# Average pooling of 2x2x2: contiguous loads of 3 MB with unequal read and write pieces in place of channel rows of 32 KB

## The chip, the cores and the metric

The kernel runs on one core of a Trainium2 chip. The metric is device microseconds (us) of one execution, median of several. A comparison of two kernels is a ratio: the mean time of one kernel's fast runs over that of the other's in the same rounds, with a 95% interval; it is therefore not quite the ratio of the medians.

## The reference

`x` is 8 x 32 x 32 x 32 x 32 float32 (33.55 MB), the output 8 x 32 x 16 x 16 x 16 (4.19 MB):

```python
window = x[:, :, d_s:d_s + 2, h_s:h_s + 2, w_s:w_s + 2]
result[:, :, i, j, k] = np.mean(window, axis=(-3, -2, -1))
```

Two neighbouring planes of 4 KB (32 x 32 floats) give one output plane of 1 KB. Any even number of planes can be pooled by itself, so a partition may hold any such piece of any channel.

## The kernel before

There are 256 channels, two sets `t` of 128, one channel per partition. A unit `k` is 1 KB of a channel (KF = 256 floats); a channel has 128 of them. A load takes 32 KB of each of 128 channels (the channels lie 128 KB apart in HBM), or twice 16 KB at the end. VectorE adds pairs along d, w and h, and the result waits in `obuf` for four stores.

```python
KF = 256
xv = x.rearrange("b c d h w -> (b c) (d h w)")
pool_in = ctx.enter_context(tc.tile_pool(name="pin", bufs=5))
obuf = [pool_out.tile([P, 16 * KF], F32, name=f"obuf{t}") for t in range(2)]
plan = [
    (0, 0, (32,)), (0, 32, (32,)), (0, 64, (32,)), (0, 96, (32,)),
    (1, 0, (32,)), (1, 32, (32,)), (1, 64, (16, 16)), (1, 96, (16, 16)),
]
def pool_unit(buf, t, k0, kb):
    # ... (cut: views)
    nc.vector.tensor_add(out=..., in0=a[:, :, 0], in1=a[:, :, 1])      # d
    nc.vector.tensor_add(out=c, in0=bv[:, :, 0], in1=bv[:, :, 1])      # w
    nc.vector.tensor_tensor_reduce(out=obuf[t][...], ...)              # h, and 1/8
for t, k0, parts in plan:
    tin = pool_in.tile([P, 32 * KF], F32, tag="tin", name="tin")
    # ... (cut: one dma_start per part, then pool_unit per part)
    nc.sync.dma_start(
        out=v, in_=xv[t * P:(t + 1) * P, (k0 + o) * KF:(k0 + o + kb) * KF])
for queue, t, k0, kb in [
    (nc.scalar, 1, 0, 2), (nc.sync, 0, 0, 16),
    (nc.sync, 1, 2, 12), (nc.sync, 1, 14, 2),
]:
    queue.dma_start(
        out=ov[t * P:(t + 1) * P, k0 * KF:(k0 + kb) * KF],
        in_=obuf[t][:, k0 * KF:(k0 + kb) * KF])
# ... (cut: the first load is moved ahead of the opening barrier, the closing
# waits for the stores are rebuilt; the change leaves both as they are)
```

## Time and profile before

| | before |
|---|---|
| median | 91.75 us (3 runs); 91.81 us in 6 runs beside the changed kernel |
| first data packet starts | 1.01 us |
| last data packet ends | 90.03 us |
| bytes moved | 33.55 MB in, 4.19 MB out |
| VectorE busy | 64.1 us of 86.6 |

The view to begin with is the DMA row of the page: it is full from the start to the end (a DMA share of 0.99 to 1.01 from 12.1 to 85.2 us), so any gain must come from making the 16 DMA engines' work smaller or their holes fewer. The profile's lines are in the prediction. Beyond the page, I use the **packet records** of the trace (start, duration, size of every packet on the 16 engines); durations of single packets and the moments of each engine's semaphore write are from there. (The semaphore writes are records of 4 bytes and 9 ns. Before there are 14 x 16 of them, so 16 for each load and store; I count one per engine, and take a transfer as landed with the last of its 16: before, that of the first load starts at 11.74, and VectorE starts on the load at 12.12. The records don't number the engines.)

### The profile page before, as it was taken

The numbers are of one execution on the slowest core, as the hardware profiler recorded it, in microseconds if no ns is written. First come the engines' busy times: TensorE is split into PE (matmuls) and PEld (weight loads), VectorE is DVE, ScalarE is ACT, GpSimd is POOL, SyncE is SP. The second block draws the span as 40 slices with busy tenths as digits, with TensorE's granted clock in tenths as the row PEclk, the third lists the DMA queues.
The fourth block names the chain that finished last, engine by engine and source line by source line (L and its number), as shares of the span: only waits on it lengthen the run. The fifth ranks groups of instructions, "written<-read, shape, count | busy, mean of one in ns | idle before, by whom it ended". The sixth has DMA issues, their size and how long they took to land.

```text
span 86.6 us, 91 instructions
## 1 busy us (share of the span) xinstructions
DVE 64.1 (74%) x40; POOL 0.2 (0%) x4
## 2 busy tenths in 40 slices
DVE  0000049993999749992999749992999999999994
POOL 0000000000000000000000000000000000000000
DMA  8889998899979999799988999699999999999999
GB/s 242 379 363 469 485 485 348 379 485 485 469 333 409 485 485 424 318 469 485 485 348 379 485 485 469 288 454 416 405 407 424 407 462 394 462 394 454 394 454 398
DMA packets 1774, 36.48 MB, mean 421 GB/s; under 512 B 192, under 2 KB 192, under 8 KB 320
## 3 DMA queue, kind: packets, MB, share of 16 engines
q1 hardware_dynamic: 1630, 36.22, 98.4%
q10 hardware_dynamic: 144, 0.26, 0.8%
HBM read 33.55 MB, written 4.19 MB: 436 GB/s over the span
## 4 chain that ended last, share of the span: by engine, by line
DMA 83%; DVE 14%; SPq 1%; issue 0%; DVEq 0%
DMA tin<-in_x_dram 83%; DVE tin L58 8%; DVE tin L62 4%; DVE obuf L65 2%; SPq L77 1%; DVE dummy L65 0%; DVEq L102 0%
## 5 line engine op out<-in xcount | busy, mean ns | idle before, releaser
L58 DVE TENSOR_TENSOR tin<-tin 128x4096 f32<-128x4096 f32 (+1 forms) x10 | 35.7, 3570 | 20.7 <-DMA tin<-in_x_dram 20.6
L62 DVE TENSOR_TENSOR tin<-tin 128x2048 f32<-128x2048 f32 (+1 forms) x10 | 18.6, 1865 | 0.3
L65 DVE CUSTOM_DVE_ANT_1 obuf<-tin 128x1024 f32<-128x1024 f32 (+1 forms) x10 | 10.1, 1011 | 0.3
L65 DVE DVE_READ_ACCUMULATOR2_ANT dummy<- 128x1 f32 x10 | 0.8, 82 | 0.0
L178 POOL MEMSET const-uint8-127<- 128x1 uint8 x1 | 0.1, 102 | 0.0
L178 POOL MEMSET const-bfloat16-1.0<- 128x1 bf16 x1 | 0.1, 101 | 0.0
L178 POOL MEMSET const-float32-0.0<- 128x1 f32 x1 | 0.1, 98 | 0.2 <-issue 0.2
L178 POOL MEMSET const-float32-1.0<- 128x1 f32 x1 | 0.1, 98 | 0.0
## 6 DMA issues: line engine op xcount, KB each, us to landing
tin<-in_x_dram SPq DMA_DIRECT2D x6, 4096.0 KB, 35.0
tin<-in_x_dram SPq DMA_DIRECT2D x4, 2048.0 KB, 38.9
out_dram<-obuf SPq DMA_DIRECT2D x1, 2048.0 KB, 36.8
out_dram<-obuf SPq DMA_DIRECT2D x1, 1536.0 KB, 8.8
out_dram<-obuf ACTq DMA_DIRECT2D x1, 256.0 KB, 9.9
out_dram<-obuf SPq DMA_DIRECT2D x1, 256.0 KB, 4.9
```

The costliest lines, as they stand in the source:

```text
L58: nc.vector.tensor_add(out=b.rearrange("p (o e) -> p o e", o=od), in0=a[:, :, 0], in1=a[:, :, 1])
L62: nc.vector.tensor_add(out=c, in0=bv[:, :, 0], in1=bv[:, :, 1])
L65: nc.vector.tensor_tensor_reduce(out=obuf[t][:, o0:o0 + od * 256].rearrange("p (j k) -> p j k", k=16), in0=cv[:, :, 0], in1=cv[:, :, 1], s ...
L77: nc.sync.dma_start(out=v, in_=xv[t * P:(t + 1) * P, (k0 + o) * KF:(k0 + o + kb) * KF])
L178: nc = _bacc.Bacc("TRN2", target_bir_lowering=False, num_devices=1)
```

## The change

The input is treated as one flat array. A load takes 3 MB in one piece, 24 KB per partition (six planes), the last 2 MB; eleven loads in place of ten, six buffers in place of five. Then, after scheduling, the access patterns of the sources are rewritten by hand: a load reads 64 rows of 48 KB, although it writes 128 rows of 24 KB; a store reads 15 or 12 KB of a partition at once, although it writes 5 or 4 pieces of 3 KB. The first load is left with 24 KB reads. The intent is fewer, larger reads per DMA engine, with the bytes unchanged.

```diff
-    pool_in = ctx.enter_context(tc.tile_pool(name="pin", bufs=5))
+    pool_in = ctx.enter_context(tc.tile_pool(name="pin", bufs=6))
     plan = [
-        (0, 0, (32,)), (0, 32, (32,)), ... (1, 96, (16, 16)),
+        (0, 24), (24, 24), (48, 24), (72, 24), (96, 24), (144, 24),
+        (120, 24), (168, 24), (192, 24), (216, 24), (240, 16),
     ]
-                out=v, in_=xv[t * P:(t + 1) * P, (k0 + o) * KF:(k0 + o + kb) * KF])
+            out=buf, in_=xf[P * k * KF:P * (k + kb) * KF].rearrange("(p e) -> p e", p=P))
-        (nc.scalar, 1, 0, 2), (nc.sync, 0, 0, 16), (nc.sync, 1, 2, 12), (nc.sync, 1, 14, 2),
+        (nc.scalar, 15, 1, 3), (nc.sync, 0, 5, 3), (nc.sync, 18, 4, 3), (nc.sync, 30, 1, 2),
     # ... (cut: destination of a store "(u p e) -> p u e", n pieces of kb units)
+    for n in copies[1:]:
+        # ... (cut)
+        if load:
+            ap = [[2 * row, 64], [1, 2 * row]]
+        else:
+            ap = [list(src.ap[0])] + [[1, 1]] * (len(src.ap) - 2) + [[1, size]]
+        if ap != [list(d) for d in src.ap]:
+            program[n] = copy.replace(i, ins=[copy.replace(src, ap=ap)], ant_dge_precooked=False)
```

More of the change, by code (lines that the diff above doesn't have):

```diff
@@ L1 @@
+import copy
 from contextlib import ExitStack
@@ L26, in pool_rows @@
     add = mybir.AluOpType.add
-    xv = x.rearrange("b c d h w -> (b c) (d h w)")
-    ov = out.rearrange("b c d h w -> (b c) (d h w)")
-    pool_in = ctx.enter_context(tc.tile_pool(name="pin", bufs=5))
+    xf = x.rearrange("b c d h w -> (b c d h w)")
+    of = out.rearrange("b c d h w -> (b c d h w)")
+    pool_in = ctx.enter_context(tc.tile_pool(name="pin", bufs=6))
     pool_out = ctx.enter_context(tc.tile_pool(name="pout", bufs=1))
-    obuf = [pool_out.tile([P, 16 * KF], F32, name=f"obuf{t}") for t in range(2)]
+    obuf = [pool_out.tile([P, kb * KF], F32, name=f"obuf{t}") for t, kb in enumerate((15, 17))]
     dummy = pool_out.tile([P, 1], F32, name="dummy")
     plan = [
-        (0, 0, (32,)),
-        (0, 32, (32,)),
-        (0, 64, (32,)),
-        (0, 96, (32,)),
-        (1, 0, (32,)),
-        (1, 32, (32,)),
-        (1, 64, (16, 16)),
-        (1, 96, (16, 16)),
+        (0, 24),
+        (24, 24),
+        (48, 24),
+        (72, 24),
+        (96, 24),
+        (144, 24),
+        (120, 24),
+        (168, 24),
+        (192, 24),
+        (216, 24),
+        (240, 16),
     ]
@@ L69, in pool_unit @@
         )
-    for t, k0, parts in plan:
-        tin = pool_in.tile([P, 32 * KF], F32, tag="tin", name="tin")
-        views = []
-        o = 0
-        for kb in parts:
-            v = tin[:, o * KF:(o + kb) * KF]
-            nc.sync.dma_start(
-                out=v, in_=xv[t * P:(t + 1) * P, (k0 + o) * KF:(k0 + o + kb) * KF])
-            views.append((v, k0 + o, kb))
-            o += kb
-        for v, k, kb in views:
-            pool_unit(v, t, k, kb)
-    for queue, t, k0, kb in [
-        (nc.scalar, 1, 0, 2),
-        (nc.sync, 0, 0, 16),
-        (nc.sync, 1, 2, 12),
-        (nc.sync, 1, 14, 2),
-    ]:
+    for k, kb in plan:
+        tin = pool_in.tile([P, 24 * KF], F32, tag="tin", name="tin")
+        buf = tin[:, :kb * KF]
+        nc.sync.dma_start(
+            out=buf, in_=xf[P * k * KF:P * (k + kb) * KF].rearrange("(p e) -> p e", p=P))
+        t = int(k >= 120)
+        pool_unit(buf, t, k - 120 * t, kb)
+    for queue, k, n, kb in [
+        (nc.scalar, 15, 1, 3),
+        (nc.sync, 0, 5, 3),
+        (nc.sync, 18, 4, 3),
+        (nc.sync, 30, 1, 2),
+    ]:
+        t = int(k >= 15)
+        o = k - 15 * t
         queue.dma_start(
-            out=ov[t * P:(t + 1) * P, k0 * KF:(k0 + kb) * KF],
-            in_=obuf[t][:, k0 * KF:(k0 + kb) * KF],
+            out=of[P * k * KF:P * (k + n * kb) * KF].rearrange("(u p e) -> p u e", u=n, p=P),
+            in_=obuf[t][:, o * KF:(o + n * kb) * KF].rearrange("p (u e) -> p u e", u=n),
         )
@@ L103 @@
     blocks = nc.main_func.blocks
-    opening, program = blocks[0].instructions, blocks[tc.starting_block_idx].instructions
+    program = blocks[tc.starting_block_idx].instructions
+    copies = [n for n, i in enumerate(program) if isinstance(i, mybir.InstDMACopy)]
+    for n in copies[1:]:
+        i = program[n]
+        src = i.ins[0]
+        load = "in_" in src.memref
+        if load:
+            row = src.ap[-1][1]
+            assert src.ap == ((row, 128), (1, row)) and row <= 24 * KF
+            ap = [[2 * row, 64], [1, 2 * row]]
+        else:
+            size = src.ap[-1][1] * (src.ap[1][1] if len(src.ap) == 3 else 1)
+            ap = [list(src.ap[0])] + [[1, 1]] * (len(src.ap) - 2) + [[1, size]]
+        if ap != [list(d) for d in src.ap]:
+            program[n] = copy.replace(i, ins=[copy.replace(src, ap=ap)], ant_dge_precooked=False)
+    opening = blocks[0].instructions
     load = next(i for i in program if isinstance(i, mybir.InstDMACopy))
```

## The prediction

> **What bounds the kernel now.** I read the page first: busy shares, the 40 slices, the byte totals and the chain of waits.
>
> ```profile
> span 86.6 us, 91 instructions
> ## 1 busy us (share of the span) xinstructions
> DVE 64.1 (74%) x40; POOL 0.2 (0%) x4
> ...
> DMA  8889998899979999799988999699999999999999
> ...
> HBM read 33.55 MB, written 4.19 MB: 436 GB/s over the span
> ## 4 chain that ended last, share of the span: by engine, by line
> DMA 83%; DVE 14%; SPq 1%; issue 0%; DVEq 0%
> ```
>
> VectorE (DVE) is idle for a quarter of the span; the DMA row is full from the first slices to the last; the chain is 83% load traffic. The 436 GB/s is slightly flattering: the span closes with the last VectorE instruction, while the last store is still moving. So I asked for stretches that run past the span (start:end, length, DVE busy, POOL busy, clock, DMA share, GB/s):
>
> ```profile
> 12.10:59.80 47.70, 39.75 (x20) 0.00 (x0) 1.00 0.99 429
> 59.80:70.50 10.70, 9.80 (x4) 0.00 (x0) 1.00 1.01 417
> 70.50:85.20 14.70, 14.32 (x16) 0.00 (x0) 1.00 1.00 428
> 85.20:90.10 4.90, 0.26 (x2) 0.00 (x0) 1.00 0.89 375
> ```
>
> The 16 DMA engines stay at a share of 0.99 to 1.01 until 85.2, and go on until the last packet record ends at 90.03. The run takes 91.75, so 1.7 us lie after the last data packet and belong to no work that this change touches. The kernel is bound by DMA engine time from 1.0 us (first packet) to 90.0 us.
>
> The packet records give that time a formula. A 32 KB packet takes 1213 ns, 16 KB 611, 12 KB 460, 2 KB 84 (medians). From the ends: (1213-84)/(32768-2048) = 0.03675 ns per byte, which leaves 8.7 ns per packet; it reproduces 611 and 460. One engine has 37.75 MB / 16 = 2.359 MB, so 86.7 us are bytes. It has 48 packets of 32 KB, 40 of 16 KB, 8 of 12 KB and 16 of 2 KB, 112 in all: 0.97 us. The 14 semaphore writes of 9 ns add 0.13. Sum 87.8 us of the 89.0 that pass from the first packet to the last. The other 1.2 are the start (the first load's data end at 11.75 instead of 1.01 + 9.70 = 10.71, 1.0 us) and uneven engines at the end.
>
> [...] 1/0.03675 = 27.2 GB/s per engine, times 16 is 435. [...] The trace has such a cost, 8.7 ns, but since every transfer before reads and writes equal pieces, it cannot tell whether reads or writes are counted. [...]
>
> **The change part by part.** Bytes don't change: 86.7 us of engine time before and after, in a queue already full. Nothing in the new layout can shorten this term while the rate is 27.2 GB/s per engine.
>
> *Pieces, per engine.* Reads: the first load keeps rows of 24 KB (8), nine loads of 3 MB have 4 reads of 48 KB each (36), the last of 2 MB has 4 of 32 KB; the four stores read 8 each (32). Sum 80. Writes: eleven loads x 8 = 88; stores 8 x (1+5+4+1) = 88. Sum 176. At 8.7 ns each:
> - if reads are counted, 80 against 112: -0.28 us;
> - if writes are counted, 176 against 112: +0.56 us.
>
> One more load adds one 9 ns semaphore write.
>
> *VectorE.* The rows by shape give the unit times:
>
> ```profile
> L58 DVE TENSOR_TENSOR tin<-tin 128x4096 f32<-128x4096 f32 x6 | 26.6, 4426 | 20.6 <-DMA tin<-in_x_dram 20.6
> L62 DVE TENSOR_TENSOR tin<-tin 128x2048 f32<-128x2048 f32 x6 | 13.8, 2292 | 0.2
> L58 DVE TENSOR_TENSOR tin<-tin 128x2048 f32<-128x2048 f32 x4 | 9.1, 2286 | 0.1
> L65 DVE CUSTOM_DVE_ANT_1 obuf<-tin 128x1024 f32<-128x1024 f32 x6 | 7.3, 1224 | 0.2
> L62 DVE TENSOR_TENSOR tin<-tin 128x1024 f32<-128x1024 f32 x4 | 4.9, 1224 | 0.1
> L65 DVE CUSTOM_DVE_ANT_1 obuf<-tin 128x512 f32<-128x512 f32 x4 | 2.8, 692 | 0.1
> ```
>
> A 24 KB row is half-way between these shapes: (4426+2286)/2 = 3356, (2292+1224)/2 = 1758, (1224+692)/2 = 958, plus 82 for the accumulator read: 6.15 us per load. A 3 MB load takes the engines 4 x (49152 x 0.03675 + 8.7) = 7.26 us, so VectorE keeps up and idles 1.1 us per load.
>
> *The end.* First load: 1.0 + 1.0 (start) + 8 x 0.912 = 9.3. The tenth: 9.3 + 9 x 7.27 + 0.97 for ScalarE's store in between = 75.7. VectorE starts 0.4 us after data (before: 11.75 and 12.12), works from 76.1 to 82.25, then on the last 2 MB unit (4.28 us) to about 86.6, against 85.46 now. The engines meanwhile finish the last load at 80.6, the 15 KB store at 85.2, the 12 KB store at 88.9. The last store is issued at 86.6 and needs about 1.0 us to its first packet (the first load's lag): 87.6, so 1.3 us of slack, where before it was 2.4 (86.5 against 88.9). VectorE's later end should be hidden.
>
> *Buffers and issues.* Six buffers of 3 MB let five loads (36 us of traffic) be queued ahead; before, four of 4 MB (39 us). Issues take 0.33 to 0.53 us now; even at twice that the second is out long before 8 us, when engines first need it.
>
> **The rivals.** (1) *Writes are counted, not reads.* For it: nothing excludes it. Against: the change forces larger reads by hand while it lets writes shrink, which its author would hardly keep if writes counted. 92.3 us. (2) *VectorE becomes the end.* For: its last instruction moves 1.1 us later. Against: 1.3 us of slack is left. If loads land a microsecond late, or the issue lag is longer than at the start, the last store starves and the time is about 92 to 92.5. (3) *Contiguous HBM reads raise the rate.* Against: packets of 32 KB all take 1211 to 1215 ns in whole loads[...]. Only the 1.0 us at the start could shrink; at best 91.0. (4) *Unequal sides make an engine stall at each piece, or HBM takes 3 KB writes badly.* Nothing in this trace speaks for it; 10% on the stores' 9.9 us would be +1.0.
>
> **Range and chances.** I take reads as counted: 91.75 - 0.28 + 0.01 = 91.5 us. Low 91.0: the read saving and half of the loss at the start. High 92.3: writes counted. Even with no packet cost and no loss at the start, 91.75 - 0.97 - 1.0 = 89.8 would barely pass the 2% line at 89.9, so faster by over 2% gets 0.02. Slower by over 2% (above 93.6) needs rival 2 and 4 together: 0.04. Within 2%: 0.94.
>
> **What the changed profile would show.** Right: a DMA share near 1.0 throughout; 3 MB loads landing 7.26 to 7.30 us apart; shapes of 3356, 1758 and 958 ns; last VectorE end near 86.6; stores as fast as before although they write 3 KB. Reads counted: 48 KB and 15 KB packet records of 1815 and 573 ns. Writes counted: 24 KB and 3 KB records (912 and 122 ns), and a load of 7.30 us. The prediction is wrong if the DMA row has holes (engines waiting for VectorE or an issue), if a load lands faster than 7.2 us after the last (above 435 GB/s), or if the first load loses much more or less than 1.0 us.

The forecast's sum came to 91.75 - 0.28 + 0.01 = 91.5 us, with the 8.7 ns per packet and the 27.2 GB/s per engine (435 for 16) worked out from the packet records of the kernel before ("such a cost" is these 8.7 ns).

## The result, and the profile after

The changed kernel takes **92.31 us** (92.10 to 92.72, 6 runs), the kernel before 91.81 (91.72 to 91.97, 6 runs): ratio 1.0058, interval 1.0035 to 1.0081. It is 0.5 us slower, not 0.25 faster.

From the changed kernel's page:

```profile
span 88.4 us, 98 instructions
## 1 busy us (share of the span) xinstructions
DVE 65.0 (73%) x44; POOL 0.2 (0%) x4
...
DMA  8899999889988999889998899989999988998999
...
HBM read 33.55 MB, written 4.19 MB: 427 GB/s over the span
## 4 chain that ended last, share of the span: by engine, by line
DMA 78%; DVE 19%; SPq 1%; issue 0%; DVEq 0%
```

The bound is the same: a full DMA row. VectorE's share of the chain rose from 14 to 19% because the page's chain is followed back from the last VectorE instruction, and before that one VectorE now works through the last two loads back to back (76.9 to 87.3, where before it was the last one alone, 81.2 to 85.5); after it the engines are still storing, so this is not the end of the program. What matters is where the engines' time went, and two stretches show it.

**The start.** The DMA row of the first 12 us, before (40 slices of 0.3 us; a packet stands in the slice in which it starts):

```profile
DMA  0009990009900990099009920992079207920592
```

and changed:

```profile
DMA  0009901099799999999999959939959993039993
```

Before, the 16 engines move in step: all start a packet in the same one or two slices, then none does. Changed, they are spread out. The packet records say how far. Before, the engines' first packets end between 2.82 and 3.27 us; changed, between 2.46 and 3.55. With the first packet at 1.01 and 8 packets each, an undelayed first load would end at 1.01 + 8 x 1.213 = 10.71 before and 1.01 + 8 x 0.912 = 8.31 changed. The slowest engine's semaphore write comes at 11.74 and 9.92: **1.03 us late before, 1.61 changed**. The spread stays: the 16 semaphore writes of a load are spread over 0.43 us in the first and the third load before, and over 1.08 to 1.09 in each of the first eight loads changed. At the end the engines finish within 0.48 us of one another before (89.54 to 90.02) and within 0.84 changed (89.80 to 90.64). The last data packet ends at 90.64 instead of 90.03, and the two profiled executions took 92.44 and 91.76.

**The loads.** VectorE waits for each load, so its first instruction per load marks the landings. Start, duration, and in brackets the idle time before it, changed kernel:

```profile
10.30 3.36 DVE L62 TENSOR_TENSOR tin<-tin 128x3072 f32<-128x3072 f32 x1 [10.30 <-DMA tin<-in_x_dram]
17.57 3.36 DVE L62 TENSOR_TENSOR tin<-tin 128x3072 f32<-128x3072 f32 x1 [1.12 <-DMA tin<-in_x_dram]
24.87 3.36 DVE L62 TENSOR_TENSOR tin<-tin 128x3072 f32<-128x3072 f32 x1 [1.15 <-DMA tin<-in_x_dram]
32.17 3.36 DVE L62 TENSOR_TENSOR tin<-tin 128x3072 f32<-128x3072 f32 x1 [1.15 <-DMA tin<-in_x_dram]
39.48 3.36 DVE L62 TENSOR_TENSOR tin<-tin 128x3072 f32<-128x3072 f32 x1 [1.15 <-DMA tin<-in_x_dram]
```

The distance is 7.27 at first, then 7.30. My two formulas gave 4 x 1815 = 7.26 with reads counted and 8 x 912 = 7.30 with writes counted, plus a semaphore write. The packet records show the same turn: records of 48 KB (they are the reads: 64 per load beside 128 rows of 24 KB written, with 16 semaphore writes per load, and the result was correct) take 1815 ns until about 25 us, then 1824 to 1829.

### The profile page after: what moved, and what is told of

It is laid out like the page before. It is cut to its first block, busy times and chain, and to the rows that moved or that the text cites. A ratio compares the mean times of both kernels' runs of the same rounds, so it can differ in the third digit from the quotient of the medians.

```text
span 88.4 us, 98 instructions
## 1 busy us (share of the span) xinstructions
DVE 65.0 (73%) x44; POOL 0.2 (0%) x4
## 4 chain that ended last, share of the span: by engine, by line
DMA 78%; DVE 19%; SPq 1%; issue 0%; DVEq 0%
DMA tin<-in_x_dram 78%; DVE tin L62 10%; DVE tin L66 5%; DVE obuf L69 3%; SPq L78 1%; DVE dummy L69 0%; DVEq L104 0%
## 5 line engine op out<-in xcount | busy, mean ns | idle before, releaser
L62 DVE TENSOR_TENSOR tin<-tin 128x3072 f32<-128x3072 f32 (+1 forms) x11 | 35.9, 3260 | 21.6 <-DMA tin<-in_x_dram 21.6
L66 DVE TENSOR_TENSOR tin<-tin 128x1536 f32<-128x1536 f32 (+1 forms) x11 | 18.8, 1710 | 0.4
L69 DVE CUSTOM_DVE_ANT_1 obuf<-tin 128x768 f32<-128x768 f32 (+1 forms) x11 | 10.3, 934 | 0.4
```

The lines of the kernel that those rows point to most:

```text
L62: nc.vector.tensor_add(out=b.rearrange("p (o e) -> p o e", o=od), in0=a[:, :, 0], in1=a[:, :, 1])
L69: nc.vector.tensor_tensor_reduce(out=obuf[t][:, o0:o0 + od * 256].rearrange("p (j k) -> p j k", k=16), in0=cv[:, :, 0], in1=cv[:, :, 1], s ...
```

## The experiments

The theory has two parts. (A) The start is wider because of **where the 16 engines begin to read**. The rows of the first load lie 128 KB apart before and 24 KB apart changed. (No run here shows which engine reads which rows, so the distance between the engines' first rows is not known; the runs with moved rows test the pitch alone.) (B) **The slower side of a transfer sets the pace**, and in the 3 MB loads that is the write side. Rivals: reads are counted after all, the start is chance, or the contiguous layout, the small stores or the widening by hand cost time in themselves.

### Undo the widening of the loads

```diff
-            ap = [[2 * row, 64], [1, 2 * row]]
+            ap = [list(d) for d in src.ap]
```

> The changed kernel, but loads 2 to 11 read rows of 24 KB (16 KB in the last) as they write them; stores as changed. 40 more reads per engine, as many writes as before. If reads are counted everywhere at 8.7 ns: +0.35 us against the changed kernel (92.3), so 92.65. If writes are counted everywhere: 92.3. My theory, that the slower side sets the pace and in the loads of 3 MB that is the write side (48 KB records of 1824 to 1829 ns against 1815): packets of 912 ns, 0.0 to 0.1 us more than changed, 92.3 to 92.4. If the slower issue of the widened second load causes the wide start: first load lands evenly, 91.9.

Measured: 92.27 us, ratio to before 1.0048 (1.0030 to 1.0066), the changed kernel 1.0058. Forty more reads per engine cost nothing that can be measured. In the trace, on the mean of the engines, loads 2 and 3 of the changed kernel took 7.25 us, load 4 7.28, and the next ones 7.30; with the widening undone loads 2 to 4 took 7.27, load 5 7.28, and the next ones 7.30. Loads 2 to 8 together took 51.00 us in both: 28 reads fewer per engine saved nothing, where 8.7 ns each would be 0.24. The slower issue is no cause of the start either: with it gone (the second load's issue takes 0.34 us, in the changed kernel 0.56), the slowest engine ended the first load at 9.91, in the changed kernel at 9.92.

### Undo the widening of the stores

```diff
-            ap = [list(src.ap[0])] + [[1, 1]] * (len(src.ap) - 2) + [[1, size]]
+            ap = [list(d) for d in src.ap]
```

> The changed kernel, but stores read pieces of 3 KB as they write them; loads as changed. 56 more reads per engine, as many writes. If the store is paced by its reads: 9 x 121.5 - 573 - 466 = 55 ns per partition, 8 partitions per engine, +0.44 us: 92.75, and packet records of 3 KB at about 121 ns. If writes pace it: 92.3, no change.

Measured: 92.34 us, ratio 1.0054 (1.0039 to 1.0068). The trace has the expected records of 121 ns, but neighbouring ones overlap (the 40 per engine of the first large store take 4.70 us, 117.6 ns each). From the last load to the last store the engines need 9.13 us on the mean, changed kernel 8.93: 0.20 more, not 0.44, for 56 reads more and the same writes. The changed kernel's own tail fits reads as well: bytes (29 KB x 8 partitions x 0.03675 = 8.73) and 24 reads at 8.7 ns make 8.94; its 80 writes at 8.7 ns would make 9.43. That reads pace the stores rests on these two traces; the times don't show it (1.0054 and 1.0058).

### Double the writes of the loads

Loads 2 to 11 write two pieces of 12 KB per partition, first with reads of 48 KB, then with reads of 12 KB:

```diff
+                i = copy.replace(i, outs=[copy.replace(dst, ap=[[step, 128], [row // 2, 2], [1, row // 2]])])
 # first:  source  [[2 * row, 64], [1, 1], [1, 2 * row]]
 # second: source  [[row, 128], [row // 2, 2], [1, row // 2]]
```

> The changed kernel, but loads 2 to 11 write two pieces of 12 KB (8 KB in the last) per partition; reads stay at 48 KB. Theory that the write side paces the loads: one piece costs 8 to 11 ns beyond its bytes, so a load of 3 MB takes 16 x (451.6 + 8 to 11) = 7.35 to 7.40 us instead of 7.30, time 92.8 to 93.3. If only reads are counted: 7.26 us each, 92.3.

> The changed kernel, but loads 2 to 11 read and write pieces of 12 KB (8 KB in the last). Theory that the slower side paces: as with 48 KB reads and 12 KB writes within 0.02 us per load, 7.37 us, time 92.8 to 93.3. If each side's pieces cost and add up: 7.37 plus 16 x 8.7 = 7.5 us, 94.5.

Measured: 92.73 us (ratio 1.0102) and 92.78 us (1.0106). VectorE's first instructions of the first of the two:

```profile
10.19 3.36 DVE L62 TENSOR_TENSOR tin<-tin 128x3072 f32<-128x3072 f32 x1 [10.19 <-DMA tin<-in_x_dram]
17.55 3.36 DVE L62 TENSOR_TENSOR tin<-tin 128x3072 f32<-128x3072 f32 x1 [1.21 <-DMA tin<-in_x_dram]
24.93 3.36 DVE L62 TENSOR_TENSOR tin<-tin 128x3072 f32<-128x3072 f32 x1 [1.23 <-DMA tin<-in_x_dram]
32.31 3.36 DVE L62 TENSOR_TENSOR tin<-tin 128x3072 f32<-128x3072 f32 x1 [1.23 <-DMA tin<-in_x_dram]
39.68 3.36 DVE L62 TENSOR_TENSOR tin<-tin 128x3072 f32<-128x3072 f32 x1 [1.22 <-DMA tin<-in_x_dram]
```

and of the second:

```profile
24.92 3.36 DVE L62 TENSOR_TENSOR tin<-tin 128x3072 f32<-128x3072 f32 x1 [1.23 <-DMA tin<-in_x_dram]
32.30 3.36 DVE L62 TENSOR_TENSOR tin<-tin 128x3072 f32<-128x3072 f32 x1 [1.23 <-DMA tin<-in_x_dram]
39.67 3.36 DVE L62 TENSOR_TENSOR tin<-tin 128x3072 f32<-128x3072 f32 x1 [1.22 <-DMA tin<-in_x_dram]
```

Both land 7.38 us apart although one makes four times the reads of the other. Only the writes are the same in both, and they are what differs from the changed kernel's 7.30. **So the writes into SBUF set the pace of these loads.** In the first run a 48 KB read, which takes 1815 ns at first, takes 1842 to 1848 in steady state.

The distances of the landings (means over the engines) also give prices; the records don't, since they overlap by some 4 ns. A load of 3 MB took 7.253 us with 4 reads per engine (changed kernel, loads 2 and 3), 7.272 with 8 (widening undone, loads 2 to 4) and 7.310 with 16 (second run here, loads 2 and 3): **4.75 ns for each further read**. Later on, where the reads no longer mattered, it took 7.304 with 8 writes and 7.379 with 16: **9.4 ns for each further write**. So with equal pieces on both sides the write side is the slower one here (9.4 against 4.75 ns).

The turn has a size, too. Adding up how much sooner than the steady distance the loads before it landed gives 0.13 us in the changed kernel, 0.12 with the widening undone, 0.13 and 0.14 in the two runs here, although the steady distance is reached with load 3 in one and with load 6 in another. It looks as if the reads can get some 0.13 us ahead of the writes and must then keep their pace; fewer reads would only use up this lead sooner. That is an interpretation; the agreement of the four numbers is what speaks for it.

### Move the first load's rows

All four give a wrong result: only the addresses that the first load reads differ. First the changed kernel with its rows 128 KB apart, then 32 KB apart:

```diff
+        if k == 0:
+            src = xf.rearrange("(c e) -> c e", e=128 * KF)[:P, :kb * KF]   # then: e=32 * KF
```

> The changed kernel, but the first load takes its 128 rows of 24 KB at a pitch of 128 KB (wrong result on purpose). Theory: the wide spread of the engines' first packets (1.45 to 2.35 us) comes from where the 16 engines start to read; then the first load's data end by 9.4 instead of 9.9 us, and the time falls by 0.4 to 0.5 us to 91.85. Rival, that the start is chance or comes from the row size or the second load's issue: 92.3 as changed.

> The changed kernel, but the first load takes its rows of 24 KB at a pitch of 32 KB instead of 24 (wrong result on purpose): nearly contiguous[...]. Theory: the wide start comes from where the 16 engines start[...]; then the slowest engine's first load ends by 9.5 (as with a pitch of 128 KB), time 92.0. Rival: contiguity as such is bad; then 9.8 or later and 92.3.

Then the kernel before with a contiguous first load (rows 32 KB apart), and with rows 24 KB apart (32 KB long, so they overlap in HBM):

```diff
+            if t == 0 and k0 == 0:
+                src = ...   # rows of kb * KF floats, one every 32 * KF; then: one every 24 * KF
```

> The kernel before, but its first load takes a contiguous range of 4 MB (wrong result on purpose). Theory of the start: first packets spread over 0.8 us or more, first load's data end 0.4 to 0.6 us later than 11.75, time 92.2 to 92.4. Rival: 91.8 as before.

> The kernel before, but the first load takes its rows of 32 KB at a pitch of 24 KB (rows overlap in HBM, wrong result on purpose)[...]. Theory: the slowest engine's first load ends 0.4 to 0.6 us later than 11.75, time 92.2. Rival, that the row size or another part of the changed program makes the wide start: 91.8 as before.

| kernel | first load's pitch | slowest engine late by | ratio to before (interval) |
|---|---|---|---|
| before | 128 KB | 1.03 us | 1 |
| before, contiguous | 32 KB | 1.23 | 0.9995 (0.9982 to 1.0008) |
| before, overlapping | 24 KB | 1.45 | 1.0033 (1.0020 to 1.0047) |
| changed | 24 KB | 1.61 | 1.0058 (1.0035 to 1.0081) |
| changed, 32 KB | 32 KB | 1.36 | 1.0025 (1.0011 to 1.0039) |
| changed, 128 KB | 128 KB | 1.01 | 1.0022 (1.0008 to 1.0036) |

("Late by" is the last engine's semaphore write of the first load in the one profile, less 1.01 us and eight packets.) For example, VectorE starts on the first load of the changed kernel at 10.30, and with a pitch of 128 KB at:

```profile
9.69 3.36 DVE L62 TENSOR_TENSOR tin<-tin 128x3072 f32<-128x3072 f32 x1 [9.69 <-DMA tin<-in_x_dram]
```

In both kernels a pitch of 24 KB costs some 0.0033 to 0.0038 of the time against 32 or 128 KB, 0.3 us; contiguity is harmless at 32 KB. Within one set of rounds the changed kernel took 92.27 and 92.34 us with 24 KB (the two runs that undo a widening) and 91.99 with 128 KB. The other profiles agree: all 17 traces sort by the first load's pitch, whatever else differs in them. The slowest engine is 0.98 to 1.03 us late with 128 KB (five traces), 1.10 to 1.36 with 32 KB (six), 1.45 to 1.61 with 24 KB (six). The pitch also sets the distance of an engine's own rows, but the delay is already there in the engines' first packets, which end 0.35 to 0.51, 0.52 to 0.72 and 0.72 to 1.09 us apart, which leaves, of what the pitch sets, where they start to read. I had expected a gain of 0.4 to 0.5 us from the profile's 0.6. The profile catches one execution: that of the 128 KB pitch took 91.78 us, the fastest of its six (median 91.99), so it overstates. Part (A) holds as far as the pitch tests it, with 0.3 us, about twice what an unaltered kernel differed by from itself (below). Why a pitch of 24 KB is worse than one of 32 or 128 KB is not shown.

### What remains: 0.2 us?

With the start mended the changed kernel is still at 1.0022 to 1.0025. I looked for it in the layout. The contiguous version with rows of 32 KB has the right start and as many load writes as before (its 4 MB loads are not widened):

```diff
-        (0, 24), (24, 24), ... (240, 16),
+        (0, 32), (32, 32), (64, 32), (96, 32), (128, 32), (160, 32), (192, 16), (208, 16), (224, 16), (240, 16),
-        (nc.scalar, 15, 1, 3), (nc.sync, 0, 5, 3), (nc.sync, 18, 4, 3), (nc.sync, 30, 1, 2),
+        (nc.scalar, 16, 1, 4), (nc.sync, 0, 4, 4), (nc.sync, 20, 1, 4), (nc.sync, 24, 3, 2), (nc.sync, 30, 1, 2),
```

> The changed kernel with rows of 32 KB in place of 24 (six contiguous loads of 4 MB, four of 2 MB; the 4 MB loads read what they write[...]; the 2 MB loads are still widened to 32 KB reads; five stores, writing 4 and 2 KB). Correct result. Theory: the loss comes from the distance of the engines' first rows[...] and from more load writes (now 80 as before), so this is as fast as the kernel before: ratio 0.998 to 1.003, 91.65 to 92.1. Rival: contiguous layout, or stores in small pieces, costs time in itself: ratio 1.005, 92.2 or more.

Measured: 92.05 us, ratio 1.0027 (1.0010 to 1.0045), inside the theory's range but not clear. So I did the halves alone (wrong results): the kernel before with contiguous loads, and with those five stores.

```diff
-                out=v, in_=xv[t * P:(t + 1) * P, (k0 + o) * KF:(k0 + o + kb) * KF])
+                out=v, in_=xf[P * (128 * t + k0 + o) * KF:P * (128 * t + k0 + o + kb) * KF].rearrange(...))
```

> The kernel before with all ten loads from contiguous ranges (rows of 32 and 16 KB, equal reads and writes) and its own stores (wrong result on purpose). With rows of 32 KB the contiguous version still was 0.27% slower than before. If the contiguous loads cause that: ratio 1.002 to 1.003, 92.0. If its stores do: 0.999 to 1.001, 91.8.

> The kernel before with its own loads, but the five stores of the contiguous version with rows of 32 KB (writes of 4 and 2 KB into contiguous ranges, ScalarE's store 512 KB; wrong result on purpose). If stores cause the remaining 0.27%: ratio 1.002 to 1.003, 92.0. If the contiguous loads do: 0.999 to 1.001, 91.8.

Measured: 91.79 us (0.9997, 0.9981 to 1.0013) and 91.87 us (1.0009, 0.9994 to 1.0024). Neither the contiguous layout nor stores in pieces of 4 and 2 KB costs anything visible. Last, the widening itself and the comparison itself:

```diff
 # rows of 32 KB, no load widened
-            ap = [[2 * row, 64], [1, 2 * row]] if row < 32 * KF else [[row, 128], [1, row]]
+            ap = [list(d) for d in src.ap]
 # first load at a pitch of 32 KB, neither loads nor stores widened: the same edit in both branches
 # the kernel before, unaltered
```

> The contiguous version with rows of 32 KB, its four 2 MB loads no longer widened (stores as there). Contiguous loads alone gave 0.9997 and the small stores alone 1.0009 against before. If the two just add up: 1.0006, 91.85, and the 0.27% of the widened version came from widening four loads. If loads and stores together cost more than each: 1.002 to 1.003, 92.0.

> The changed kernel with its first load at a pitch of 32 KB (wrong result on purpose) and no read widened, neither of loads nor of stores. With widened reads the same was 1.0025. If widening is what costs the rest: 1.000 to 1.001, 91.85. If the rest is the 24 KB writes (8 more per engine at about 10 ns) and chance: 1.0015 to 1.003, 92.0; 24 reads more in the stores could add up to 0.2.

> The kernel before, unaltered, against itself in the same rounds: what the comparison gives where nothing differs. Ratio 1.000, interval about 0.0015 to either side; if it is off by 0.002, differences of 0.2% in the other runs can't be told from chance.

Measured: 91.83 us (1.0009, 0.9995 to 1.0023); 92.04 us (1.0037, 1.0020 to 1.0054); and the kernel before **against itself 1.0016 (1.0003 to 1.0030)**. The last is the most useful: an identical kernel comes out 0.16% slower, and its interval leaves out 1. So 0.0022 to 0.0027 lie at the edge of what this comparison can tell, and I settle nothing on them. The second says that widening is not what costs it, since without it the ratio is no lower. The write count leaves room for a part: 88 load writes per engine against 80, at 9.4 ns, are 0.08 us (an estimate from the runs above).

One source of such scatter is in nearly every trace: at 77 to 81 us, in the last load, some packets take 0.1 to 0.8 us longer than bytes and piece price explain. Summed per engine (packets over 60 ns late, divided by 16) this is 0.43 us in the changed kernel. In the two profiles of the kernel before, of identical code, it is 0.05 and 0.52; the first has another 0.27 at 60 to 64 us, the second 0.05. What it is stays open; the two runs with 12 KB writes didn't have it.

### A try for something better

In its first profile the kernel before loses 0.26 us beside ScalarE's small store, so I moved that store's bytes to the SP queue:

```diff
-        (nc.scalar, 1, 0, 2),
         (nc.sync, 0, 0, 16),
-        (nc.sync, 1, 2, 12),
+        (nc.sync, 1, 0, 14),
         (nc.sync, 1, 14, 2),
```

> The kernel before with its four stores made three, all on the SP queue (16, 14 and 2 KB rows; ScalarE's store of 2 KB goes into the second). In the trace before, two loads of 2 MB beside ScalarE's store took 10.71 us where their own 16 packets of 611 ns and eight of 84 make 10.45. Theory: those 0.26 us and eight packets' 8.7 ns (0.07) are saved, 91.5. Rival: the store costs only its bytes: 91.75.

Measured: 91.98 us, ratio 1.0035 (1.0014 to 1.0056): a miss. Without the store the 2 MB loads did land 4.89 us apart, as expected, but the last of them took 5.41, with the slow packets just described (0.49 us per engine). And the 0.26 us were no property of that store: in the second profile of the kernel before, the two loads beside it took 10.47 us against the sum of 10.45. No run beat the kernel before by more than the noise (lowest ratio 0.9995). Larger pieces on both sides were not run.

## Why the prediction was wrong

- **Within 2% of the kernel before: right** (1.0058); only the direction inside these 2% was wrong.
- **Bound, bytes, buffers: right.** The DMA engines are the limit in both kernels, and none of the holes I had named (waiting for VectorE or for an issue) appeared.
- **VectorE: right.** Predicted 3356, 1758 and 958 ns; the changed kernel's rows by shape:

```profile
L62 DVE TENSOR_TENSOR tin<-tin 128x3072 f32<-128x3072 f32 x10 | 33.6, 3358 | 21.6 <-DMA tin<-in_x_dram 21.6
L66 DVE TENSOR_TENSOR tin<-tin 128x1536 f32<-128x1536 f32 x10 | 17.6, 1758 | 0.3
L69 DVE CUSTOM_DVE_ANT_1 obuf<-tin 128x768 f32<-128x768 f32 x10 | 9.6, 958 | 0.3
```

- **VectorE's end:** predicted 86.6, came at 87.27, late by the late loads. It stayed hidden: with 1.0 us from issue to first packet it is 88.3, and the first engine reached the last store at 89.1.
- **"If reads are counted, 80 against 112: -0.28 us": the step that failed.** I took a transfer's cost as bytes plus one price per piece of one side, and chose the reads because the change enlarges them. In the runs both sides have a price and in the loads the slower side sets the pace, the writes into SBUF: in steady state 7.30 us with 24 KB writes whatever the reads, 7.38 with 12 KB writes whatever the reads. (In the stores it seems to be the reads.) Of the 0.28 us nothing was seen, neither in the time nor in the sum of the loads (51.00 us with and without widened reads). The price was too high as well: 8.7 ns from the lengths of records, 4.75 per read from the landings.
- **The kernel before had shown a sign of it.** I wrote that 32 KB packets all take 1211 to 1215 ns in whole loads. Of those that start after 31 us, 95 of 372 take longer, up to 1266, and the loads land 9.68 us apart at first (loads 2 and 3) but 9.71 for load 5. That looks like the same turn to the pace of the writes; no run tests it in that kernel.
- **The test I proposed could not tell.** I wrote that records of 1815 and 573 ns would show reads to be counted, and a load of 7.30 us writes. Both appeared. A record is a read whichever side paces (48 KB records beside writes of 24 and of 12 KB); only the distance of the landings tells.
- **"1.0 + 1.0 (start) + 8 x 0.912": the term that was too small.** I carried the start's loss over from a load at another pitch. It was 1.61 in the profile, and the excess was some 0.3 us in the timed comparisons that undo or provoke it. A first load that loses much more than 1.0 us was among my signs of being wrong. I had allowed that only a smaller start was possible under "contiguous HBM reads".
- **Rival 1 named 92.3, but for a reason that is only half right:** it put 0.56 us on writes, most of them the stores' 3 KB pieces, and those cost nothing visible (the tail of 8.93 us fits reads alone; a store reading 12 KB and writing four of 3 KB settled at 466 ns per read, against 460 with one write of 12 KB). That its number fits is luck.
- From 91.5 to 92.31 are 0.8 us: the saving that did not come (0.28) and the wider start (0.3) make 0.6; the last 0.2 us are little more than the 0.0016 (0.15 us) by which identical kernels differed, and their cause stays open.

## What to carry to other kernels

Where the DMA engines are the limit, count the pieces of both sides of each transfer and look for the slower side; enlarging the pieces of one side alone bought nothing here, because the other set the pace (7.30 us per load with reads of 48 and of 24 KB). Take the price of a piece from the distance of landings (4.75 ns per read), not from the length of records (8.7). Look at when each of the 16 engines finishes, not only at their mean: the changed kernel's spread of 1.08 us in the first load was still there in the eighth and 0.84 at the end, and the pitch of the first load's rows was worth 0.3 us. And run the old kernel against itself before explaining two parts in a thousand.
